# Masks first and 64-row heads in turn over two banks, in a fused attention and expert kernel on one Trainium2 core

## The chip, the cores and the metric

The kernel runs on one NeuronCore of a Trainium2 chip. The metric is the device time of one execution in microseconds (us); smaller is better. The engines are named as in the profile: PE is TensorE (PEld its weight loads), DVE is VectorE, ACT is ScalarE, POOL is GpSimd and SP is SyncE, which here issues the transfers of weights. SBUF is the memory on the core, PSUM the eight banks that PE writes its results to.

## What is computed

Two transformer blocks over 256 tokens of width 1024, in float32. The first has three attention branches on one normed input: A (8 heads of 64, each query keeps the 64 keys that a separate index scores highest), B (8 heads of 96, causal) and M (4 heads of 128, over a memory). The second has a differential attention, a gated linear attention in chunks of 64 tokens, a cross attention and a mixture of 32 experts. Cut to the parts that the change touches:

```python
# branch A: index, top 64 keys, masked attention
dots = einsum('bqhc,bsc->bhqs', q_i, k_i) * 64 ** -0.5
index = einsum('bhqs,bqh->bqs', relu(dots), w_i * 8 ** -0.5)
_, idx = top_k(where(causal, index, -1e30), 64)
p = softmax(where(kept, einsum('bqhd,bkhd->bhqk', q_a, k_a) * 64 ** -0.5, -1e30))
# linear attention, per chunk of 64 tokens
a = where(lower, einsum(q * e_pos, k * e_neg), einsum(q * e_neg, k * e_pos))
# differential attention: the mask lets a token see its own chunk of 64 and those before
p = softmax(where(mask, q1 @ k1 * s, -inf)) - lam * softmax(where(mask, q2 @ k2 * s, -inf))
```

## The kernel before

Tokens lie in two tiles of 128 rows, t = 0 and 1. Every dense product runs through one stream (`Stream`): its order is a list of names (`ORDER`), its weights come in pieces of 1 MB through SP into a pool of 23 slots, and each piece is split into a high and a low part (ACT at L165, DVE at L166) before PE multiplies it. `pump()` places one unit of that work, as a rule 12 matmuls of 512 columns (L214), and the splits of units ahead. The order of the work on each engine is the order in which the code is written: attention code calls `pump` or `fill` at fixed places to put units between its own steps, and lists such as `fills([3, 5, 1, ...])` say how many units go after each step.

An attention works on units `(t, heads, keys)`. Stage 1 (`s1`, or `d1` in the differential attention) writes the scores of a unit into one PSUM bank of 512 columns (tag `sc`, of which there are two) and calls `exps`: a maximum on DVE (L624), its negation (L625), then one exponential per head on ACT (L628). Stage 2 transposes the result on PE (L640) and copies it (L642), stage 3 multiplies it with the values (L674, L1563). A mask is added to the scores by one more matmul, the stationary `negid` (-1e30 on the diagonal) times a mask of zeros and ones (`add_mask`, L685).

Four places have a contraction of 64 rows, where a head lies either in rows 0 to 63 or in rows 64 to 127 of the operand: the index scores (`idx1`, L1093), the scores of branch A (`scores_a`, L1182), the chunk products of the linear attention (L1464), and the differential attention (`d1`, L1538, its two maps in the two halves). In the first two, `causal_units(2)` gives units whose heads all lie in one half:

```python
return [(t, hs, (t + 1) * P) for t in (1, 0) for hs in groups(8, 512 // ((t + 1) * P), step)]
```

`scores_a` and `d1` write one head's scores and then that head's mask. Ahead of branch A, `branch_input("B", ysb)` transposes the result of branch B through both `sc` banks (L543), with evictions on ACT (L526) and DVE (L527). After the dense part come the experts: their weights pass through the same slots, four experts at a time in strips of 32 rows (L1848, L1880).

Of the kernel before, what the change touches and what calls it, by code (L numbers as in the profile page):

```python
# [322 lines left out]
def block_kernel(ctx: ExitStack, tc: tile.TileContext, a: dict, out: bass.AP):  # L323
# [308 lines left out]
    on_act = [0, 0]  # L632

# [11 lines left out]
    def attention(units, fill, scores, rs, vals, close, heads, dv, out_heads=None):  # L645
# [38 lines left out]
    def add_mask(out_ap, mask):  # L684
        PE.matmul(out_ap, lhsT=negid, rhs=mask, start=False, stop=True)  # L685
# [77 lines left out]
    chmask = masks_bf[:, 0:P]  # L763
    POOL.memset(chmask, 0.0)
    POOL.memset(chmask[0:64, 64:128], 1.0)
# [322 lines left out]
    def idx1(u):  # L1088
        t, hs, nk = u
        sc = ps([P, len(hs), nk], "sc")  # L1090
        for i, hd in enumerate(hs):
            p0 = 64 * (hd % 2)
            PE.matmul(sc[:, i, :], lhsT=qiT[p0:p0 + 64, hd // 2, t * P:(t + 1) * P],  # L1093
                      rhs=kiT[p0:p0 + 64, 0, 0:nk], start=True, stop=True)
        rl = et([P, len(hs), nk])
        on_act[1] += 2
        if on_act[1] >= 4:
            on_act[1] -= 4
            DVE.tensor_scalar(rl, sc, 0.0, None, op0=OP.max)
        else:  # L1100
            ACT.activation(rl, sc, AF.Relu)
        relus[id(u)] = rl

    def idx2(u):
        t, hs, nk = u
        rl = relus.pop(id(u))
        for i, hd in enumerate(hs):
# [29 lines left out]
    pipeline(causal_units(2), (idx1, idx2), fills([1, 0, 2, 3, 0, 2, 0]))  # L1137
# [23 lines left out]
    def scores_b(t, hd, nk, dst):  # L1161
        PE.matmul(dst, lhsT=qbT[0:96, hd, t * P:(t + 1) * P], rhs=kbT[0:96, hd, 0:nk], start=True, stop=False)
        add_mask(dst[:, nk - P:], noncausal)
# [36 lines left out]
    def scores_m(t, hd, nk, dst):  # L1200
        PE.matmul(dst, lhsT=qmT[:, hd, t * P:(t + 1) * P], rhs=kmT[:, hd, :], start=True, stop=True)
# [38 lines left out]

    lq = st([P, 4, 64], "wk")
# [213 lines left out]
    for t in range(NT):  # L1455
        aT = et([P, 2, 2, P])
        POOL.memset(aT, 0.0)
        ats[t] = aT
        for par in range(2):
            pa = ps([P, 2, 2, P], "sc")  # L1460
            p0 = 64 * par
            for f, (ki, qi) in enumerate(((3, 0), (2, 1))):
                for hp in range(2):
                    PE.matmul(pa[:, f, hp, :], lhsT=gqa[p0:p0 + 64, ki, hp, t * P:(t + 1) * P],  # L1464
                              rhs=gqa[p0:p0 + 64, qi, hp, t * P:(t + 1) * P], start=True, stop=True)
            for f, m in enumerate((mlow, mup)):
                DVE.copy_predicated(aT[:, par], m[:, None, :].to_broadcast([P, 2, P]), pa[:, f])
# [56 lines left out]

# [3 lines left out]
    def d1(u):  # L1528
# [4 lines left out]
        es = []  # L1533
# [504 lines left out]
```

## Time and profile before

| | |
|---|---|
| three runs | 1045.23, 1046.37, 1047.03 us, median 1046.37 us |
| the profiled execution | 1044.64 us, of which the span of its instructions is 1042.9 us |
| PE busy | 930.0 us (89%) |
| DVE, ACT, POOL busy | 445.5, 333.8, 112.5 us |
| mean bandwidth from memory | 278 GB/s over the span |

The span runs from the first to the last instruction; the device time has 1.7 us more around it. A matmul's busy time runs to its modelled end, which lies behind the start of the next one, so that lengths on PE are read here from start to start. The granted clock of PE is given as a share of 2.4 GHz: 1.00 is 2.4 GHz, 0.50 is 1.2 GHz. A stretch has the columns busy time (and count) for each engine, then the clock, the share of the transfer engines that is busy, and GB/s.

### The profile page before, as it was taken

How to read it: one execution, taken by the hardware profiler on the slowest of the kernel's cores; microseconds unless marked ns; L12 is line 12 of the kernel's file. 1: busy time of each engine (PE TensorE's matmuls, PEld its weight loads, DVE VectorE, ACT ScalarE, POOL GpSimd, SP SyncE). 2: the span in 40 equal slices, each digit the busy share in tenths (PEclk: the TensorE clock that was granted, in tenths of full speed). 3: DMA queues.
4: the chain of work that ended last, by engine and by line, in shares of the span. 5: the costliest groups of instructions: out<-in, count | busy, mean ns of one | idle time of the engine just before them, and what ended most of it. 6: DMA issues, size and time to landing. Idle time of an engine off the chain costs nothing.

```text
span 1042.9 us, 12833 instructions
## 1 busy us (share of the span) xinstructions
PE 930.0 (89%) x5073; PEld 622.4 (60%) x5073; DVE 445.5 (43%) x814; ACT 333.8 (32%) x637; POOL 112.5 (11%) x156
## 2 busy tenths in 40 slices
PE   8999999999999999999999999877878687787876
PEld 8978877788888887877887853413232141422323
DVE  5689775476676666766765421101000010100002
ACT  6556565355534573445654200000000000000000
POOL 4354000020132011310002000000000000000000
PEclk9999999999999999999999999989989898988978
DMA  6933344345473732463578989999999999999997
GB/s 221 385 127 120 112 152 145 117 163 166 157 228 108 231 120 94 165 219 105 200 279 293 354 332 418 420 421 418 420 419 419 421 419 420 419 419 420 420 407 241
DMA packets 88316, 289.85 MB, mean 278 GB/s; under 512 B 5841, under 2 KB 20030, under 8 KB 66750
## 3 DMA queue, kind: packets, MB, share of 16 engines
q1 hardware_dynamic: 87294, 286.46, 72.4%
q0 software_dynamic: 960, 2.55, 0.9%
q8 instruction: 41, 0.67, 0.3%
q14 instruction: 21, 0.17, 0.0%
HBM read 287.94 MB, written 1.05 MB: 277 GB/s over the span
## 4 chain that ended last, share of the span: by engine, by line
PE 51%; DMA 38%; DVE 6%; ACT 2%; SPq 1%; issue 1%; POOL 0%; ACTq 0%; POOLq 0%; DVEq 0%
PE pg L214 36%; DMA s<-in_w_e_up_dram 13%; DMA s<-in_w_e_down_dram 12%; DMA s<-in_w_e_gate_dram 11%; DVE s L166 2%; PE po L674 2%; PE psc L1848 2%; PE psc L543 1%; PE psc L1182 1%; PE ptp L640 1%; PE psc L1538 1%; SPq L143 1%; PE psc L1880 1%; DVE s L577 1%; PE psc L685 1%
## 5 line engine op out<-in xcount | busy, mean ns | idle before, releaser
L214 PE MATMUL pg<-s,s 128*128 128x512 f32 (+5 forms) x2076 | 454.2, 376 | 4.0 <-ACT s L165 1.8
L214 PEld LDWEIGHTS pg<-s,s 128*128 128x128 f32 x2076 | 365.9, 189 | 71.0 <-ACT s L165 2.5
L1848 PE MATMUL psc<-s,wk 128*32 128x512 f32 (+1 forms) x1024 | 180.0, 697 | 63.3 <-DMA s<-in_w_e_up_dram 38.9
L166 DVE TENSOR_TENSOR s<-s,s 128x1024 fp32r<-128x1024 f32 (+4 forms) x170 | 197.0, 1190 | 49.3 <-ACT s L165 49.0
L165 ACT ACTIVATE s<-s 128x1024 fp32r<-128x1024 f32 (+4 forms) x170 | 160.8, 995 | 13.0 <-DVE s L166 7.6
L1848 PEld LDWEIGHTS psc<-s,wk 128*32 128x32 f32 x1024 | 41.3, 127 | 195.2 <-issue 76.0
L1880 PE MATMUL psc<-s,wk 128*32 128x512 f32 (+1 forms) x576 | 71.0, 571 | 10.8 <-DMA s<-in_w_e_down_dram 10.4
L1855 DVE SCALAR_TENSOR_TENSOR wk<-wk,psc 128x512 f32<-128x512 f32 x8 | 5.5, 687 | 135.3 <-ACT wk L1854 135.3
L1872 ACT ACTIVATE wk<-ptp 128x512 f32<-128x512 f32 (+1 forms) x9 | 4.9, 550 | 172.4 <-PE ptp L1871 172.4
L1859 DVE TENSOR_TENSOR wk<-wk,psc 128x512 f32<-128x512 f32 (+1 forms) x8 | 5.2, 654 | 120.6 <-PE psc L1848 120.6
L628 ACT ACTIVATE s<-psc,sm,tiny 128x256 f32<-128x256 f32 (+1 forms) x64 | 32.9, 520 | 72.1 <-DVE sm L625 71.5
L494 POOL TENSOR_TENSOR sm<-sm,tiny 128x8 f32<-128x8 f32 (+2 forms) x28 | 36.0, 1299 | 179.5 <-DVE sm L498 146.4
L1880 PEld LDWEIGHTS psc<-s,wk 128*32 128x32 f32 x576 | 20.1, 116 | 55.6 <-issue 32.4
L1805 PE MATMUL ptp<-masks,h 128*128 128x128 f32 x128 | 30.3, 398 | 12.7 <-DVE masks L1792 12.7
L1805 PEld LDWEIGHTS ptp<-masks,h 128*128 128x128 f32 x128 | 28.6, 311 | 19.1 <-issue 17.5
L1854 ACT ACTIVATE wk<-psc 128x512 f32<-128x512 f32 x8 | 4.8, 597 | 109.6 <-PE psc L1848 109.6
L1885 DVE COPY wk<-psc 128x512 f32<-128x512 f32 (+1 forms) x10 | 6.1, 611 | 68.5 <-PE psc L1880 68.5
L624 DVE TENSOR_REDUCE sm<-psc 128x2 f32<-128x512 f32 (+1 forms) x26 | 17.9, 689 | 32.6 <-PE psc L685 23.6
L1892 PE MATMUL pg<-wk,wr 128*128 128x512 f32 (+1 forms) x72 | 30.2, 559 | 0.0
L1805 PE MATMUL po<-masks,h 128*128 128x128 f32 x120 | 28.2, 388 | 0.0
L1805 PEld LDWEIGHTS po<-masks,h 128*128 128x128 f32 x120 | 27.6, 320 | 0.0
L1887 ACT ACTIVATE wk<-psc 128x512 f32<-128x512 f32 (+1 forms) x8 | 4.6, 570 | 71.3 <-PE psc L1880 71.3
(328 smaller groups left out, 805.1 us busy)
## 6 DMA issues: line engine op xcount, KB each, us to landing
s<-in_w_e_gate_dram SPq DMA_DIRECT2D x64, 1024.0 KB
s<-in_w_e_up_dram SPq DMA_DIRECT2D x64, 1024.0 KB
s<-in_w_e_down_dram SPq DMA_DIRECT2D x60, 1024.0 KB
s<-in_w_in_dram SPq DMA_DIRECT2D x36, 1024.0 KB
s<-in_w_ckv_dram SPq DMA_DIRECT2D x8, 1024.0 KB
s<-in_w_branch_dram SPq DMA_DIRECT2D x6, 1024.0 KB
s<-in_w_mem_kv_dram SPq DMA_DIRECT2D x4, 1024.0 KB
s<-in_w_out_dram SPq DMA_DIRECT2D x4, 1024.0 KB
```

The source lines that it names most:

```text
L143: dma(out=self.loads[x][1][part], in_=self.loads[x][0][part])
L165: self.k.nc.scalar.activation(hl[:, 0], w, AF.Copy)
L166: self.k.nc.vector.tensor_tensor(out=hl[:, 1], in0=w, in1=hl[:, 0].bitcast(F32), op=OP.subtract)
L214: mm(j.outs[t], lhsT=x_, rhs=hl[:, int(c == 2), i, :], start=step == ends[t][0], stop=step == ends[t][1])
L494: POOL.tensor_tensor(out=dst, in0=src, in1=e_.to_broadcast(shape), op=OP.pow)
L624: DVE.tensor_reduce(out=mx, in_=sc, axis=AX.X, op=OP.max)
L628: ACT.activation(e[:, i, :], sc[:, i, :], AF.Exp, bias=nb[:, i:i + 1], scale=rs[:, c:c + 1], accum_out=sums[:, c:c + 1])
L674: PE.matmul(o[:, hd % (out_heads or heads), :], lhsT=pt[:, i * nkt + kt, :], rhs=vals(kt, hd), start=(kt == 0), stop=(kt == nkt - 1))
L1805: PE.matmul(tp[:, kb - k0, :], lhsT=src, rhs=sel[:, t], start=(t == 0), stop=(t == 1))
L1848: PE.matmul(p_[s0:s0 + sn, :], lhsT=xs[k0 // 4][:, kb, s0:s0 + sn], rhs=rows(m, i, k0 + kb, cols), start=(k0 + kb == 0), stop=(k0 + kb == 7))
L1880: PE.matmul(p_[s0:s0 + sn, :], lhsT=hT[:, kb, s0:s0 + sn], rhs=rows(2, i, kb, slice(c * 512 + cols.start, c * 512 + cols.stop)), start=(kb ...
L1892: PE.matmul(outs[t][c], lhsT=sgT[:, t, :], rhs=od, start=start, stop=stop)
```

## The change

Index scores: the heads of a pair of units lie in the two halves, and each matmul goes to the other unit's bank than the one before it. Branch A: the same pairing; the mask of a whole bank is written first by one matmul of 512 columns, and the scores are added to it; two units of weight products are placed between the transposes of branch B's result and the first mask, and the numbers of units between the steps are others. Linear attention: the two halves in turn, into two banks. Differential attention: both masks first, over all keys in place of the last 128, then the scores of the two maps in turn. The chunk mask, now of 256 columns, is built by POOL after branch M in place of at the start. In the other attentions the scores functions take another form with the same matmuls.

```diff
-    def add_mask(out_ap, mask):
-        PE.matmul(out_ap, lhsT=negid, rhs=mask, start=False, stop=True)
+    def begin_mask(out_ap, mask):
+        n, nk = out_ap.shape[1:]
+        PE.matmul(out_ap, lhsT=negid, rhs=mask[:, None, :].to_broadcast([P, n, nk]), start=True, stop=False)
+
+    def in_turn(banks):
+        for i in range(len(banks[0])):
+            for b, items in enumerate(banks):
+                yield b, i, items[i], i + 1 == len(items)
...
         def s1(u):
-            t, hs, nk = u
+            if index[id(u)] % at_once:
+                return
+            us = units[index[id(u)]:index[id(u)] + at_once]
+            t, _, nk = u
...
-            sc = ps([P, len(hs), nk], "sc")
-            for i, hd in enumerate(hs):
-                scores(t, hd, nk, sc[:, i, :])
-            live[id(u)] = exps(sc, rs[t], hs, per_t[t][1])
+            scs = [ps([P, len(hs), nk], "sc") for _, hs, _ in us]
+            scores(t, [hs for _, hs, _ in us], nk, scs)
+            for x_, sc in zip(us, scs):
+                live[id(x_)] = exps(sc, rs[t], x_[1], per_t[t][1])
...
-    chmask = masks_bf[:, 0:P]
-    POOL.memset(chmask, 0.0)
-    POOL.memset(chmask[0:64, 64:128], 1.0)
...
+    def paired_units():
+        for t in (1, 0):
+            n = 4 // (t + 1)
+            for h0 in range(0, 8, 2 * n):
+                for par in range(2):
+                    yield t, list(range(h0 + par, h0 + 2 * n, 2)), (t + 1) * P
...
-    pipeline(causal_units(2), (idx1, idx2), fills([1, 0, 2, 3, 0, 2, 0]))
+    pu = list(paired_units())
+    pipeline([pu[i:i + 2] for i in range(0, len(pu), 2)], (idx1, idx2), fills([2, 2, 2, 2]))
...
-    def scores_a(t, hd, nk, dst):
-        p0 = 64 * (hd % 2)
-        PE.matmul(dst, lhsT=qaT[p0:p0 + 64, hd // 2, t * P:(t + 1) * P], rhs=kaT[p0:p0 + 64, hd // 2, 0:nk],
-                  start=True, stop=False)
-        add_mask(dst, amask[t][:, 0:nk])
+    def scores_a(t, banks, nk, outs):
+        for o in outs:
+            begin_mask(o, amask[t][:, 0:nk])
+        for b, i, hd, end in in_turn(banks):
+            p0 = 64 * (hd % 2)
+            PE.matmul(outs[b][:, i, :], lhsT=qaT[p0:p0 + 64, hd // 2, t * P:(t + 1) * P],
+                      rhs=kaT[p0:p0 + 64, hd // 2, 0:nk], start=False, stop=end)
 
     branch_input("B", ysb)
+    begun_at = W.next_mm
+    while W.next_mm < begun_at + 2:
+        fill()
+
...
-    attention(causal_units(2), fills([3, 5, 1, 1, 2, 4, 0, 2]), scores_a, rs_a, values_a,
-              closer(ysa, pair_of("zya", 0), 8, 64, r1), 8, 64)
+    attention(list(paired_units()), fills([3, 2, 3, 1, 3, 2, 0, 1]), scores_a, rs_a, values_a,
+              closer(ysa, pair_of("zya", 0), 8, 64, r1), 8, 64, at_once=2)
...
+    chmask = masks_bf[:, 0:S]
+    POOL.memset(chmask, 0.0)
+    POOL.memset(chmask[0:64, S - 64:], 1.0)
...
+        pas = [ps([P, 2, 2, P], "sc") for _ in range(2)]
+        pieces = [(f, hp, ki, qi) for f, (ki, qi) in enumerate(((3, 0), (2, 1))) for hp in range(2)]
+        for par, _, (f, hp, ki, qi), _ in in_turn([pieces, pieces]):
+            p0 = 64 * par
+            PE.matmul(pas[par][:, f, hp, :], lhsT=gqa[p0:p0 + 64, ki, hp, t * P:(t + 1) * P],
+                      rhs=gqa[p0:p0 + 64, qi, hp, t * P:(t + 1) * P], start=True, stop=True)
...
-        es = []
-        for m in range(2):
-            sc = ps([P, n, nk], "sc")
+        hs = list(range(h0, h0 + n))
+        scs = [ps([P, n, nk], "sc") for _ in range(2)]
+        for sc in scs:
+            begin_mask(sc, chmask[:, S - nk:])
+        for m, i, hd, end in in_turn([hs, hs]):
             p0 = 64 * m
-            for i in range(n):
-                PE.matmul(sc[:, i, :], lhsT=dqT[p0:p0 + 64, h0 + i, t * P:(t + 1) * P],
-                          rhs=dkT[p0:p0 + 64, h0 + i, 0:nk], start=True, stop=False)
-                add_mask(sc[:, i, nk - P:], chmask)
-            es.append(exps(sc, rs_d[t][:, m:8:2], list(range(h0, h0 + n)), dsum[t][:, m, :]))
+            PE.matmul(scs[m][:, i, :], lhsT=dqT[p0:p0 + 64, hd, t * P:(t + 1) * P], rhs=dkT[p0:p0 + 64, hd, 0:nk],
+                      start=False, stop=end)
+        es = [exps(scs[m], rs_d[t][:, m:8:2], hs, dsum[t][:, m, :]) for m in range(2)]
```

On PE at the start of branch A, before: `s_199` is branch B's result, `psc` the score banks, `pg` the product banks, and a trailing number tells one buffer from another.

```order
L543 MATMUL psc_1639<-ident,s_199_1151 128x128 x4
L543 MATMUL psc_1644<-ident,s_199_1151 128x128 x4
L1182 MATMUL psc_1659<-s_168_1026 128x256
L685 LDWEIGHTS negid
L685 MATMUL psc_1659<-masks,negid 128x256
L1182 MATMUL psc_1659<-s_168_1026 128x256
L685 LDWEIGHTS negid
L685 MATMUL psc_1659<-masks,negid 128x256
L214 MATMUL pg_1675<-s_273_1566,s_269_1537 128x512 x3
L214 MATMUL pg_1676<-s_273_1566,s_269_1537 128x512 x3
```

In the changed kernel, from the last rows of the second of two product units that now stand between those transposes and the first mask (its last operand `s_269` is the memory, as in the last rows above):

```order
L214 MATMUL pg_1661<-s_278_1601,s_269_1535 128x512 x3
L214 MATMUL pg_1662<-s_278_1601,s_269_1535 128x512 x3
L688 LDWEIGHTS negid
L688 MATMUL psc_1693<-masks,negid 128x512
L688 LDWEIGHTS negid
L688 MATMUL psc_1694<-masks,negid 128x512
L1198 MATMUL psc_1693<-s_168_1024 128x256
L1198 MATMUL psc_1694<-s_168_1024 128x256
L1198 MATMUL psc_1693<-s_168_1024 128x256
L1198 MATMUL psc_1694<-s_168_1024 128x256
```

The product units that stood behind the first scores are ahead of them, and four heads share one visit to the score banks.

On PE at the first unit of the differential attention, before: `s_635` holds its queries and keys.

```order
L1538 MATMUL psc_4104<-s_635_3836 128x256
L685 LDWEIGHTS negid
L685 MATMUL psc_4104<-masks,negid 128x128
L1538 MATMUL psc_4104<-s_635_3836 128x256
L685 LDWEIGHTS negid
L685 MATMUL psc_4104<-masks,negid 128x128
L1538 MATMUL psc_4115<-s_635_3836 128x256
L685 LDWEIGHTS negid
L685 MATMUL psc_4115<-masks,negid 128x128
```

The same place in the changed kernel:

```order
L688 LDWEIGHTS negid
L688 MATMUL psc_4094<-masks,negid 128x512
L688 LDWEIGHTS negid
L688 MATMUL psc_4095<-masks,negid 128x512
L1561 MATMUL psc_4094<-s_635_3826 128x256
L1561 MATMUL psc_4095<-s_635_3826 128x256
L1561 MATMUL psc_4094<-s_635_3826 128x256
L1561 MATMUL psc_4095<-s_635_3826 128x256
L214 MATMUL pg_4065<-s_668_3996,s_383_2177 128x512 x3
L214 MATMUL pg_4066<-s_668_3996,s_383_2177 128x512 x3
```

Both masks come first and the scores alternate. As before, one unit of twelve product matmuls, of which the first two rows stand here, separates this unit from the next, whose two masks need both banks again.

## Rows read from the trace of the kernel before

**Rows 1.** The page: busy time of PE, share of the span, instructions.

```profile
PE 930.0 (89%) x5073; PEld 622.4 (60%) x5073; DVE 445.5 (43%) x814; ACT 333.8 (32%) x637; POOL 112.5 (11%) x156
```

**Rows 2.** Stretches of the span: PE, PEld, DVE, ACT, POOL, clock, transfers, GB/s.

```profile
480.00:612.00 132.00, 127.25 (x749) 101.76 (x752) 75.33 (x166) 58.66 (x132) 10.96 (x18) 1.00 0.73 261
612.00:1042.00 430.00, 333.36 (x1912) 132.03 (x1904) 42.75 (x80) 16.75 (x32) 0.00 (x0) 0.90 1.00 409
```

**Rows 3.** SP's waits from 480 to 613 us: total, times, longest.

```profile
SPq L135 <- PE pg L214: 61.1, 15, 8.1
...
SPq L135 <- DMA s<-in_w_e_gate_dram: 0.2, 1, 0.2
```

**Rows 4.** Timeline of PE at the index scores: start, length, engine, line.

```profile
51.12 1.13 PE L1093 MATMUL psc<-s,s 64*128 64x256 f32 x4
52.18 3.01 PE L214 MATMUL pg<-s,s 128*128 128x512 f32 x12
55.12 1.14 PE L1093 MATMUL psc<-s,s 64*128 64x256 f32 x8
56.26 5.79 PE L214 MATMUL pg<-s,s 128*128 128x512 f32 x24
...
63.04 8.45 PE L214 MATMUL pg<-s,s 128*128 128x512 f32 x36
71.42 1.71 PE L1093 MATMUL psc<-s,s 64*128 64x128 f32 x16
73.06 0.64 PE L590 MATMUL ptp<-ident,s 128*96 128x128 f32 x4
```

**Rows 5.** Timeline of PE at branch A; in brackets its idle time before.

```profile
153.01 1.03 PE L543 MATMUL psc<-ident,s 128*128 128x128 f32 x8
156.07 0.67 PE L1182 MATMUL psc<-s 64*128 64x256 f32 x2 [2.03 <-DVE s L527]
...
157.96 9.60 PE L214 MATMUL pg<-s,s 128*128 128x512 f32 x36
167.49 0.70 PE L1182 MATMUL psc<-s 64*128 64x256 f32 x2
...
169.07 0.60 PE L640 MATMUL ptp<-ident,s 128*128 128x128 f32 x4
...
194.80 0.48 PE L1182 MATMUL psc<-s 64*128 64x128 f32 x2
...
197.01 0.61 PE L640 MATMUL ptp<-ident,s 128*128 128x128 f32 x4
```

**Rows 6.** A stretch of branch A, with the clock behind POOL's column.

```profile
157.04:160.45 3.41, 3.41 (x9) 2.28 (x10) 0.85 (x2) 1.12 (x5) 0.00 (x0) 0.50 0.23 84
```

**Rows 7.** Timeline of DVE and of PE at the linear attention's chunk products.

```profile
414.07 1.72 DVE L1467 COPY_PREDICATED s<-s,psc 128x256 f32<-128x256 int32 x4 [1.79 <-PE psc L1464]
...
412.80 1.71 PE L1464 MATMUL psc<-s 64*128 64x128 f32 x16
415.13 1.93 PE L1464 MATMUL psc<-s 64*128 64x128 f32 x16 [0.61 <-DVE s L1467]
416.99 1.30 PE L1473 MATMUL po<-s,s 128*128 128x128 f32 x10
```

**Rows 8.** Timeline of all engines at the differential attention.

```profile
466.71 0.67 PE L1538 MATMUL psc<-s 64*128 64x256 f32 x2 [0.62 <-DVE s L577]
...
468.36 0.69 DVE L624 TENSOR_REDUCE sm<-psc 128x2 f32<-128x512 f32 x1 [1.80 <-PE psc L685]
...
469.34 0.56 ACT L628 ACTIVATE s<-psc,sm,tiny 128x256 f32<-128x256 f32 x1 [2.38 <-DVE sm L625]
...
469.71 3.01 PE L214 MATMUL pg<-s,s 128*128 128x512 f32 x12
...
471.92 0.20 ACT L628 ACTIVATION_READ_ACCUMULATOR s<-psc,sm,tiny 128x1 f32 x1
...
478.99 0.48 PE L1538 MATMUL psc<-s 64*128 64x128 f32 x2
...
483.50 0.61 PE L640 MATMUL ptp<-ident,s 128*128 128x128 f32 x4
```

**Rows 9.** Timeline of PE in the cross attention.

```profile
551.61 1.56 PE L1618 MATMUL psc<-s,s 128*128 128x256 f32 x6 [1.79 <-ACT s L579]
```

More of the change, by code (lines that the diff above doesn't have):

```diff
@@ L643, in weights_T, with attention @@
         return pt
-    def attention(units, fill, scores, rs, vals, close, heads, dv, out_heads=None):
+    def attention(units, fill, scores, rs, vals, close, heads, dv, out_heads=None, at_once=1):
         live = {}
@@ L1086, in causal_units, with idx1, idx2 @@
         return [(t, hs, (t + 1) * P) for t in (1, 0) for hs in groups(8, 512 // ((t + 1) * P), step)]
[L1088 to L1091, printed above, removed]
+    def paired_units():
[4 more added lines that the diff above has]
+                    yield t, list(range(h0 + par, h0 + 2 * n, 2)), (t + 1) * P
+    def idx1(us):
+        t, nk = us[0][0], us[0][2]
+        scs = [ps([P, len(hs), nk], "sc") for _, hs, _ in us]
+        for b, i, hd, _ in in_turn([hs for _, hs, _ in us]):
             p0 = 64 * (hd % 2)
-            PE.matmul(sc[:, i, :], lhsT=qiT[p0:p0 + 64, hd // 2, t * P:(t + 1) * P],
+            PE.matmul(scs[b][:, i, :], lhsT=qiT[p0:p0 + 64, hd // 2, t * P:(t + 1) * P],
                       rhs=kiT[p0:p0 + 64, 0, 0:nk], start=True, stop=True)
[L1095 to L1107, printed above, removed]
+        relus[id(us)] = [et([P, len(hs), nk]) for _, hs, _ in us]
+        ACT.activation(relus[id(us)][0], scs[0], AF.Relu)
+        DVE.tensor_scalar(relus[id(us)][1], scs[1], 0.0, None, op0=OP.max)
+    def idx2(us):
+        t, nk = us[0][0], us[0][2]
+        rls = relus.pop(id(us))
+        for b, i, hd, _ in in_turn([hs for _, hs, _ in us]):
+            rl = rls[b]
             w_ = wi[:, t, hd:hd + 1]
@@ L1159, in block_kernel, with scores_b @@
     qbT, kbT, vb = place["qbT"], place["kbT"], pair_of("vbz", 0)
-    def scores_b(t, hd, nk, dst):
-        PE.matmul(dst, lhsT=qbT[0:96, hd, t * P:(t + 1) * P], rhs=kbT[0:96, hd, 0:nk], start=True, stop=False)
-        add_mask(dst[:, nk - P:], noncausal)
+    def scores_b(t, banks, nk, outs):
+        for _, i, hd, _ in in_turn(banks):
+            dst = outs[0][:, i, :]
+            PE.matmul(dst, lhsT=qbT[0:96, hd, t * P:(t + 1) * P], rhs=kbT[0:96, hd, 0:nk], start=True, stop=False)
+            PE.matmul(dst[:, nk - P:], lhsT=negid, rhs=noncausal, start=False, stop=True)
     def values_b(kt, hd):
@@ L1198, in block_kernel, with scores_m @@
     kmT, qmT, vm = place["kqm"][:, 0], place["kqm"][:, 1], pair_of("vzm", 0)
-    def scores_m(t, hd, nk, dst):
-        PE.matmul(dst, lhsT=qmT[:, hd, t * P:(t + 1) * P], rhs=kmT[:, hd, :], start=True, stop=True)
+    def scores_m(t, banks, nk, outs):
+        for _, i, hd, _ in in_turn(banks):
+            PE.matmul(outs[0][:, i, :], lhsT=qmT[:, hd, t * P:(t + 1) * P], rhs=kmT[:, hd, :], start=True, stop=True)
     attention([(t, hs, S) for t in range(NT) for hs in groups(4, 2, 1)], fills([3, 0, 3, 1, 1, 4]), scores_m, rs_m,
@@ L1458, in block_kernel @@
         ats[t] = aT
-        for par in range(2):
[L1460 to L1465, printed above, removed]
+        pas = [ps([P, 2, 2, P], "sc") for _ in range(2)]
[4 more added lines that the diff above has]
+                      rhs=gqa[p0:p0 + 64, qi, hp, t * P:(t + 1) * P], start=True, stop=True)
+        for par in range(2):
             for f, m in enumerate((mlow, mup)):
-                DVE.copy_predicated(aT[:, par], m[:, None, :].to_broadcast([P, 2, P]), pa[:, f])
+                DVE.copy_predicated(aT[:, par], m[:, None, :].to_broadcast([P, 2, P]), pas[par][:, f])
     for t in range(NT):
@@ L1614, in block_kernel, with scores_x @@
     ox = {}
-    def scores_x(t, hd, nk, dst):
-        for b in range(2):
-            PE.matmul(dst, lhsT=qxT[:, 2 * hd + b, t * P:(t + 1) * P], rhs=kxT[:, 2 * hd + b, :],
-                      start=(b == 0), stop=(b == 1))
+    def scores_x(t, banks, nk, outs):
+        for _, i, hd, _ in in_turn(banks):
+            for b in range(2):
+                PE.matmul(outs[0][:, i, :], lhsT=qxT[:, 2 * hd + b, t * P:(t + 1) * P], rhs=kxT[:, 2 * hd + b, :],
+                          start=(b == 0), stop=(b == 1))
     def close_x(t, hs, o, sums):
```

1 line of the change is left out of this document (removed).

## The prediction

> **What bounds the kernel now.** I began with the page, for the engine that is never free: PE is busy for 930 of 1042.9 us [rows 1]. Cut into stretches, the span has two regimes [rows 2]. From 480 to 612 us PE works 127 of 132 us at full clock while the transfer engines are busy 73%; from 612 us on, those engines are busy all the time, at 409 GB/s, and PE is not. So the first part is PE's, the second belongs to the experts' weights. Whether time saved early reaches the end is read from SP's waits before 613 us [rows 3]: SP waits for PE's products, 61.1 us in total, and for an earlier transfer only 0.2. Weights are fetched when PE frees a slot, so if PE reaches 612 us earlier by x, the saturated stretch begins and ends earlier by x. A change on PE is therefore worth what it moves PE's clockwork before 612 us, no more. For that I read PE's timeline from start to start, and beside it DVE and ACT, since a score bank is free only after its exponentials.
>
> **Term 1, the index scores.** A unit of four matmuls of 256 columns, all in one half, lasts from 51.12 to the product at 52.18, 1.06 us. Where two units of different halves stand next to each other, eight of them last from 55.12 to 56.26, 1.14 us [rows 4]: the halves work at the same time, and PE already does this by itself where the code lets it. The last two units, sixteen matmuls of 128 columns, last from 71.42 to 73.06, 1.64. With the other single unit (like the first) the present cost is 1.06 + 1.14 + 1.06 + 1.64 = 4.9 us. Afterwards there are three visits, each of two halves: 3 x 1.14 = 3.4. I take **-1.5 us**; if the last pair stays at 1.64 it is -1.0, and as a product after a visit starts slowly too and one visit goes, -2.0 is the other end.
>
> The Trainium skill, page "TensorE: Matmul & The Clock Gate", section "Part 3: Packing small matmuls", says that matmuls start and end strictly in program order. These rows differ: the code has all of one half first, yet both halves finish together. By the rule the present kernel would have no overlap here, and this term would be about 1 us larger, the time 1032 us.
>
> **Term 2, branch A.** Three things go.
> - The gap. After the transposes of branch B's result PE stands still for 2.03 us, until DVE has emptied the last score bank [rows 5]. The change puts two product units there (twelve matmuls each, 8.38 / 3 = 2.8 us by the 36 from 63.04 to 71.42 [rows 4]). Their weights were split before the gap, since they run right after the first scores now. -2.0; 0 if they wait after all.
> - The clock. Right behind that gap the granted clock is 0.50, that is 1.2 GHz, for 3.41 us [rows 6]; the 36 product matmuls from 157.96 take 9.53 us [rows 5] where the same number takes 8.38 [rows 4]. With the gap filled I expect no fall: -1.2, or 0. A gap of 1.79 us in the cross attention [rows 9] stands in a stretch at 1.00 [rows 2].
> - The masks and the halves. The units cost 1.89 (156.07 to 157.96), three times 1.58 (167.49 to 169.07, two more like it), and twice 2.21 (194.80 to 197.01 and its like) [rows 5]: 11.05 us. A unit of 1.58 is four scores of 1.06 as above and 0.52 for its masks and changes of shape. Afterwards a pair of units has two masks of 512 columns and eight scores. The mask columns are as many as before (8 x 256 + 8 x 128 = 6 x 512), so two masks cost at most 2 x 0.52, and at least two streams of 512 columns, 2 x 0.23 by the product rows; near the lower end, 0.55, since one change of shape is left of several. With 1.14 for the scores a pair costs 1.7, three pairs 5.1. **-5.9**, between -4.5 (dear masks) and -6.4.
>
> No new wait follows here: between two pairs stand five and four product units, 14 and 11 us, while four exponentials take ACT about 3 us (below) and a split 1. Where the list now holds 2 + 15 units in place of 18, one unit runs later and nothing is saved or lost. Branch A together: **-9.1 us**.
>
> **Term 3, the linear attention.** Sixteen matmuls of each tile of tokens shrink as above, but PE is not what sets the pace. DVE's four copies begin at 414.07, when the first bank is done, and take 1.72 [rows 7]. The second tile needs both banks at once: its second half cannot start before the fourth copy ends at 415.8, and then needs about 1.1 us, to 416.9. Now the next matmul starts at 416.99. So **0**: PE's gain turns into a wait of some 1.9 us in place of 0.61. Bounds: -1.2 if nothing waits (3.6 us of scores [rows 7] against two visits of 1.2), +1.7 if the wait halves the clock for one stretch as in [rows 6].
>
> **Term 4, the differential attention.** The first unit takes 466.71 to 469.71, 3.0 us, the second the same within 0.1, the third 478.99 to 483.50, 4.5 [rows 8]: 10.5 us, against three pairs of 1.7 by term 2 (the wider masks are in that). On PE alone that is -5.4. But only one product unit of 2.8 us stands between two visits, and each visit now wants both banks. The exponentials start at 469.34 and end at 472.12 [rows 8]; the maximum before them starts at 468.36, and both banks would be written by 468.4, so this chain begins no earlier than now. PE would be back at 466.71 + 1.7 + 2.8 = 471.2 and wait some 1.3 us for the second bank. The second visit's chain also begins where DVE is free, as now, so there is a like wait before the third, and 0.6 us at the single transpose bank. Of 5.4 about 2.6 goes into these waits: **-2.8 us**, between 0 (the chain takes all) and -5.4 (no wait).
>
> The Trainium skill, page "TensorEngine Tiling (Array Packing)", section "PSUM Bottleneck", speaks against the change: tiling speeds up TensorE, but not the emptying of PSUM. Rows 7 and 8 agree with it in these two places; rows 5 do not show it in branch A.
>
> **What costs nothing.** The two POOL fills of the chunk mask move behind branch M; POOL is busy 11% of the span [rows 1], and the last mask matmul of branch A, which they overwrite, is long past. Scores of branches B, M and of the cross attention are the same instructions.
>
> **Sum.** -1.5 - 9.1 + 0 - 2.8 = -13.4 us. The profiled execution took 1044.64 us, 1.7 more than its span, and is 1.7 below the median of the runs shown, so 1031.2 on its scale is **1033.0 us** on that of the median. Small ends: -1.0 - 4.5 + 1.7 + 0 = -3.8, or 1042.6. Large ends: -2.0 - 9.6 - 1.2 - 5.4 = -18.2, or 1028.2.
>
> **The rivals.**
> - Banks bind in branch A too: PE arrives at both banks before the exponentials have left them, and the 5.9 there shrinks as the 5.4 did, to about half, with term 4 at half of its 2.8: 13.4 - 3.0 - 1.4 = 9.0, some less if the filled gap reappears before the first mask; 1037 to 1040 us. For it: both banks of two are claimed at once. Against: 11 us and more of products between the pairs.
> - Slower: turning between the halves costs what a change of shape costs. Now two units of 0.52 hold two masks each; their 512 columns stream in 0.23, which leaves 0.14 for each mask's going and coming. The new code turns at every score, 64 times (16 in each of the four places). Without overlap branch A would give 3.3 for its masks and 3.2 for gap and clock, the differential attention 3, the index scores and chunks would lose 1.3: -8.2. At 0.14 a turn 64 turns cost 9.0, and it breaks even near 0.13; at 0.2 it ends 4.6 slower, 1051 us. Against it: eight in 1.14 us [rows 4].
> - The freed time does not reach the end because the weights come no sooner: 1045 to 1047. Against it stand SP's waits [rows 3].
> - More than forecast: no wait in terms 3 and 4, 1029 us. Against it: only one product unit between the visits.
>
> **How the numbers follow.** About 0.2% (2 us) is what a measurement of this kernel can tell from no change. Forecast with its bounds 0.66, banks binding in branch A 0.18, more than forecast 0.07, nothing reaching the end 0.05, slower 0.04. The first three are all faster by over 2 us: 0.91; same 0.05; slower 0.04. The likeliest case is 1033.0. From 1029.0 to 1041.0 lie the forecast with most of its bounds, the first rival and the lower edge of the fourth, some 0.85; I leave the last 0.05 for terms that I have not seen.
>
> **What would show it.** Right: no stretch at half clock at branch A, and products in place of the 2.03 us gap; eight scores in 1.1 to 1.2 us in the index, branch A and the differential attention; PE idle for one to two microseconds before the second and third visit of the latter, and for about 2 before the second tile of the linear attention; the saturated stretch of transfers beginning 12 to 15 us earlier than 612 us and as long as before. Wrong: scores of two halves one after the other, PE waiting for a score bank in branch A, or PE early at 590 us and the stream of weights no earlier.

## The result, and the profile after

The changed kernel takes 1032.61 us (median of four runs, 1031.90 to 1034.28), the kernel before 1046.28 (four runs, 1045.23 to 1047.03): a ratio of 0.9869, with a 95% interval from 0.9836 to 0.9901. The forecast was 1033.0, between 1029.0 and 1041.0. The two profiled executions lie closer together than the medians: 1044.64 us before (span 1042.9), below the lowest of its four runs, and 1034.28 after (span 1032.6), its longest run. About 3 us of the changed kernel's profiled time lie in two stretches at half clock, below; whether its other executions have them too is not shown. One of E6's six runs below took 1260.51 us, at a mean granted clock of 0.645; without it E6's median is 1031.69 in place of 1031.75.

The page of the changed kernel, busy time by engine, which answers to [rows 1]:

```profile
PE 911.8 (88%) x5053; PEld 614.5 (60%) x5053; DVE 445.3 (43%) x814; ACT 333.4 (32%) x637; POOL 113.7 (11%) x156
```

The two microseconds in which the transfer engines become busy, first in the kernel before, with the columns of [rows 2]:

```profile
605.00:607.00 2.00, 2.00 (x21) 0.53 (x17) 0.35 (x1) 0.00 (x0) 0.00 (x0) 1.00 0.75 295
```

The same in the changed kernel, and its saturated stretch:

```profile
595.00:597.00 2.00, 2.00 (x24) 0.65 (x20) 0.00 (x0) 0.00 (x0) 0.00 (x0) 1.00 0.95 401
602.00:1032.00 430.00, 326.61 (x1908) 131.32 (x1900) 42.77 (x80) 16.77 (x32) 0.00 (x0) 0.92 1.00 408
```

SP's waits from 470 to 603 us, as in [rows 3]:

```profile
SPq L135 <- PE pg L214: 54.2, 14, 6.6
```

PE's busy time fell by 18 us, of which 7 lie in the saturated stretch (333.4 to 326.6 us), where PE does not set the pace. In the 5 us ahead of the windows shown, the transfer engines are busy 9% before and 10% after, so they saturate some 10 us earlier. The end of the span comes 10.3 us earlier too, and the saturated stretch is as long as in [rows 2], 430 us at 408 GB/s: what PE gains ahead of it reaches the end, as the forecast said. SP still waits for PE's products there.

Where the time went is read from the start of the same PE instruction in both traces. The shift is after minus before.

| stage | before, from and to | after, from and to | change in the stage |
|---|---|---|---|
| index scores | 51.12, 73.06 | 51.15, 72.68 | -0.4 |
| branch A, to the first score of branch M | 153.01, 238.67 | 152.59, 228.70 | -9.5 |
| linear attention, to its next product unit | 412.80, 419.09 | 402.85, 410.68 | +1.5 |
| differential attention, to the cross attention | 466.71, 543.67 | 458.22, 531.35 | -3.8 |
| cross attention, to its second transposes | 543.67, 553.45 | 531.35, 542.73 | +1.6 |
| the rest, to the end of the span | 553.45, 1042.9 | 542.73, 1032.6 | +0.4 |

Timeline of the changed kernel at the index scores, on PE:

```profile
51.15 1.13 PE L1107 MATMUL psc<-s,s 64*128 64x256 f32 x8
52.22 3.01 PE L214 MATMUL pg<-s,s 128*128 128x512 f32 x12
56.29 3.06 PE L214 MATMUL pg<-s,s 128*128 128x512 f32 x12 [1.06 <-ACT s L915]
59.28 1.14 PE L1107 MATMUL psc<-s,s 64*128 64x256 f32 x8
66.01 1.16 PE L1107 MATMUL psc<-s,s 64*128 64x128 f32 x16
```

The same on ACT, the first evictions after that visit:

```profile
55.41 0.46 ACT L913 ACTIVATE s<-pg,tiny 128x256 f32<-128x256 f32 x1
55.77 0.47 ACT L915 ACTIVATE s<-pg,tiny 128x256 f32<-128x256 f32 x1
```

The three visits take 1.07, 1.06 and 1.09 us (3.2; the four of before took 4.9), but a new wait of 1.06 us has come between the two product units after the first visit. The second unit needs a product bank that ACT begins to empty only at 55.41. Before, ACT began to empty that bank at nearly the same time, 55.38, but the visit at 55.12 [rows 4] lay across that moment, and PE went on at 56.26 without a wait.

Timeline of PE at branch A:

```profile
153.38 5.70 PE L214 MATMUL pg<-s,s 128*128 128x512 f32 x24
158.92 0.60 PE L688 MATMUL psc<-masks,negid 128*128 128x512 bf16 x2
159.45 1.13 PE L1198 MATMUL psc<-s 64*128 64x256 f32 x8
160.52 8.46 PE L214 MATMUL pg<-s,s 128*128 128x512 f32 x36
...
190.05 0.60 PE L688 MATMUL psc<-masks,negid 128*128 128x512 bf16 x2
190.59 1.16 PE L1198 MATMUL psc<-s 64*128 64x128 f32 x16
191.68 0.66 PE L638 MATMUL ptp<-ident,s 128*128 128x128 f32 x4
```

The stretch of [rows 6], with the clock behind POOL's column:

```profile
157.04:160.45 3.41, 3.41 (x19) 2.15 (x18) 1.68 (x2) 0.24 (x1) 0.00 (x0) 1.00 0.92 283
```

The gap of 2.03 us in [rows 5] is filled, no stretch is at half clock, and a pair takes 1.60 us (158.92 to 160.52): 0.53 for two masks and 1.07 for eight scores. The three pairs take 1.60, 1.60 and 1.63, together 4.8 in place of 11.05. No wait for a bank stands anywhere in branch A.

Timeline of PE and DVE at the linear attention:

```profile
402.85 1.16 PE L1486 MATMUL psc<-s 64*128 64x128 f32 x16
404.11 1.72 DVE L1490 COPY_PREDICATED s<-s,psc 128x256 f32<-128x256 int32 x4 [1.79 <-PE psc L1486]
405.18 0.46 PE L1486 MATMUL psc<-s 64*128 64x128 f32 x2 [1.16 <-DVE s L1490]
405.98 1.70 PE L1486 MATMUL psc<-s 64*128 64x128 f32 x14 [0.35 <-DVE s L1490]
407.61 2.27 PE L1496 MATMUL po<-s,s 128*128 128x128 f32 x10
```

The two stretches at half clock that the changed kernel has between 14 and 600 us:

```profile
406.36:409.77 3.41, 3.41 (x23) 2.96 (x21) 1.66 (x4) 0.00 (x0) 0.00 (x0) 0.50 0.25 39
539.48:542.89 3.41, 3.41 (x9) 2.59 (x10) 0.17 (x1) 0.85 (x3) 3.38 (x5) 0.50 1.05 387
```

PE waits 1.16 us for DVE's copies of the first bank and 0.35 for those of the second, and right behind that the clock is at 0.50 for 3.41 us. The other fall stands behind the gap of 1.8 us in the cross attention, which [rows 9] has too, there at full clock.

Timeline of PE at the differential attention, with the last exponential of the first visit on ACT:

```profile
458.22 0.77 PE L688 MATMUL psc<-masks,negid 128*128 128x512 bf16 x2 [0.53 <-DVE s L577]
458.92 1.13 PE L1561 MATMUL psc<-s 64*128 64x256 f32 x8
...
462.71 0.56 ACT L628 ACTIVATE s<-psc,sm,tiny 128x256 f32<-128x256 f32 x1
462.84 0.39 PE L688 MATMUL psc<-masks,negid 128*128 128x512 bf16 x1
463.41 0.38 PE L688 MATMUL psc<-masks,negid 128*128 128x512 bf16 x1 [0.19 <-ACT s L628]
468.04 0.39 PE L688 MATMUL psc<-masks,negid 128*128 128x512 bf16 x1
469.13 0.38 PE L688 MATMUL psc<-masks,negid 128*128 128x512 bf16 x1 [0.70 <-ACT s L628]
471.10 0.66 PE L638 MATMUL ptp<-ident,s 128*128 128x128 f32 x4 [0.51 <-DVE s L640]
```

The waits are where the forecast put them, at the second bank of the second and third visit and at the transpose bank, but they are 0.2, 0.7 and 0.5 us long.

### The profile page after: what moved, and what is told of

Read it like the earlier page. It is cut to its first block, busy times and chain, and to the rows that moved or that the text cites. A ratio compares the mean times of both kernels' runs of the same rounds, so it can differ in the third digit from the quotient of the medians.

```text
span 1032.6 us, 12784 instructions
## 1 busy us (share of the span) xinstructions
PE 911.8 (88%) x5053; PEld 614.5 (60%) x5053; DVE 445.3 (43%) x814; ACT 333.4 (32%) x637; POOL 113.7 (11%) x156
## 3 DMA queue, kind: packets, MB, share of 16 engines
q1 hardware_dynamic: 87294, 286.46, 73.1%
## 4 chain that ended last, share of the span: by engine, by line
PE 49%; DMA 38%; DVE 8%; ACT 2%; SPq 1%; issue 1%; POOL 0%; ACTq 0%; POOLq 0%; DVEq 0%
PE pg L214 36%; DMA s<-in_w_e_up_dram 13%; DMA s<-in_w_e_down_dram 12%; DMA s<-in_w_e_gate_dram 12%; DVE s L166 2%; PE psc L1871 2%; PE po L675 2%; PE psc L543 1%; ACT s L628 1%; DVE s L577 1%; PE ptp L638 1%; PE psc L1641 1%; PE psc L1903 1%; SPq L143 1%; PE ptp L1828 1%
## 5 line engine op out<-in xcount | busy, mean ns | idle before, releaser
L1871 PE MATMUL psc<-s,wk 128*32 128x512 f32 (+1 forms) x1024 | 172.3, 660 | 67.2 <-DMA s<-in_w_e_up_dram 43.2
L1903 PE MATMUL psc<-s,wk 128*32 128x512 f32 (+1 forms) x576 | 71.9, 559 | 12.9 <-DMA s<-in_w_e_down_dram 12.6
```

The costliest lines, as they stand in the source:

```text
L1871: PE.matmul(p_[s0:s0 + sn, :], lhsT=xs[k0 // 4][:, kb, s0:s0 + sn], rhs=rows(m, i, k0 + kb, cols), start=(k0 + kb == 0), stop=(k0 + kb == 7))
L1903: PE.matmul(p_[s0:s0 + sn, :], lhsT=hT[:, kb, s0:s0 + sn], rhs=rows(2, i, kb, slice(c * 512 + cols.start, c * 512 + cols.stop)), start=(kb ...
```

## The experiments

Each is one edit of the changed kernel (E1: of the kernel before). E1 to E4 were measured together, E0 and E5 to E7 together, and E8 and E9 together. From one such group to the next the median of the same kernel moves by one to two microseconds (the kernel before 1046.02 to 1047.94, the changed kernel 1032.61 and 1033.74), so that small things are read from the traces. For E1 to E4 the changed kernel stands in another group, at 1032.61.

**E1, the product units ahead, alone.**

```diff
     branch_input("B", ysb)
+    begun_at = W.next_mm
+    while W.next_mm < begun_at + 2:
+        fill()
...
-    attention(causal_units(2), fills([3, 5, 1, 1, 2, 4, 0, 2]), scores_a, rs_a, values_a,
+    attention(causal_units(2), fills([3, 3, 1, 1, 2, 4, 0, 2]), scores_a, rs_a, values_a,
```

> The kernel before, with only the two product units put ahead of branch A's first scores and taken from the five behind the second unit. Theory: the gap of 2.03 us and the stretch at half clock behind it (1.2 us) go and the units keep their lengths (1.58, 2.21 us): 3.2 us less than before, about 1043. Rival one: the gap only moves, since the units taken from between the scores no longer cover the exponentials; a like gap of 1 to 2 us stands before a transpose, and the gain is 1 to 2 us. Rival two: the fall of the clock was not the gap's; a stretch at half clock stays in branch A and the gain is 2.0.

Measured: 1041.74 us against 1046.62 for the kernel before in the same group, ratio 0.996 (0.9942 to 0.9979): 4.9 us less by the medians, 4.2 by the ratio. Timeline of PE at branch A in E1:

```profile
159.86 0.70 PE L1182 MATMUL psc<-s 64*128 64x256 f32 x2
...
161.37 8.47 PE L214 MATMUL pg<-s,s 128*128 128x512 f32 x36
```

The gap and the half clock are gone from branch A, and the first unit takes 1.51 us where it took 1.89. From the transposes to 70 us later the trace gives 4.0 us; up to 0.46 of it is another wait, ahead of the transposes at 226.0 us, that is no longer in the trace. The other 3.6 are the gap (2.0), the clock on the 36 products (1.1) and the clock on the first unit (0.4), which the theory had left out. No gap moved elsewhere, so the theory stands. The profiled execution also has a stretch at half clock from 478.30 to 485.13 us, in the differential attention. PE's last idle time ahead of it ended 15 us earlier, and the kernel before ran the same code at full clock; so this fall has no gap at all, and the gain is read from branch A alone.

**E7, the changed kernel without the units ahead.**

```diff
     branch_input("B", ysb)
-    begun_at = W.next_mm
-    while W.next_mm < begun_at + 2:
-        fill()
...
-    attention(list(paired_units()), fills([3, 2, 3, 1, 3, 2, 0, 1]), scores_a, rs_a, values_a,
+    attention(list(paired_units()), fills([5, 2, 3, 1, 3, 2, 0, 1]), scores_a, rs_a, values_a,
```

> The changed kernel without the two product units ahead of branch A (five units behind the first pair in place of three). Theory: PE waits for branch B's last eviction again, 2.0 us ahead of the first mask, so 2.0 us slower than the changed kernel, 3.2 where the half clock comes with the gap, as in the kernel before. Rival: with masks first the wait matters less, since the first mask needs one bank only and the scores wait for the second: the gap shrinks to 1.2 us or less.

Measured: 1035.30 us, 1.6 more than the changed kernel in the same group (E0). Timeline of PE behind the gap:

```profile
154.87 0.94 PE L688 MATMUL psc<-masks,negid 128*128 128x512 bf16 x2 [1.94 <-DVE s L527]
...
157.75 14.30 PE L214 MATMUL pg<-s,s 128*128 128x512 f32 x60
```

The stretch that begins there, with its clock:

```profile
155.17:158.58 3.41, 3.41 (x12) 2.02 (x12) 0.70 (x2) 0.00 (x0) 0.00 (x0) 0.50 0.41 155
```

The gap comes back with 1.94 us, and the half clock with it; the first pair takes 2.88 us in place of 1.60. From the transposes to the first score of branch M E7 takes 3.1 us more than the changed kernel, 3.65 without a wait for a transfer that only the latter has (0.59 us). The medians show less than the 3.2 us that were expected; in the profiled execution E7's linear attention runs at full clock, which takes off 1.5 (E0). In the two kernels that have this gap, the clock fell behind it; in the ten others that were profiled, it did not fall here. The rival that masks first would shorten the gap falls.

**E3, masks first but halves apart, in branch A.**

```diff
-    attention(list(paired_units()), fills([3, 2, 3, 1, 3, 2, 0, 1]), scores_a, rs_a, values_a,
-              closer(ysa, pair_of("zya", 0), 8, 64, r1), 8, 64, at_once=2)
+    attention(causal_units(2), fills([3, 3, 1, 1, 2, 4, 0, 2]), scores_a, rs_a, values_a,
+              closer(ysa, pair_of("zya", 0), 8, 64, r1), 8, 64)
```

> The changed kernel with branch A's units unpaired again (one half, one bank at a time), each with one mask of 512 columns first. It splits the saving of branch A's score units (11.05 us before, 4.8 now) into masks and halves. Theory: a unit of 256 columns takes 1.06 for its scores and 0.4 for its mask, a unit of 128 columns 1.1 and 0.4: 4 x 1.46 + 2 x 1.5 = 8.8, so 4.0 us slower than the changed kernel (3.4 to 4.5): two thirds of the saving are the halves'. Rival: the masks' changes of shape were the larger part: units of 1.1 to 1.2, 1.5 to 2 us slower than the changed kernel.

Measured: 1036.49 us, 3.9 more than the changed kernel. Timeline of PE in E3, one unit of each width:

```profile
169.23 0.39 PE L688 MATMUL psc<-masks,negid 128*128 128x512 bf16 x1
169.55 1.13 PE L1198 MATMUL psc<-s 64*128 64x256 f32 x4
170.61 0.66 PE L638 MATMUL ptp<-ident,s 128*128 128x128 f32 x4
...
190.35 0.39 PE L688 MATMUL psc<-masks,negid 128*128 128x512 bf16 x1
190.67 1.16 PE L1198 MATMUL psc<-s 64*128 64x128 f32 x8
191.76 0.66 PE L638 MATMUL ptp<-ident,s 128*128 128x128 f32 x4
```

A unit takes 1.38 (256 columns) or 1.41 us (128 columns): 4 x 1.38 + 2 x 1.41 = 8.3. Of the 6.2 us that the units give, 0.4 are the clock's (the first unit, 1.89 - 1.51 in E1), 10.7 - 8.3 = 2.3 the masks' and 8.3 - 4.8 = 3.5 the halves'. Four scores of one half take the 1.06 us that eight of both halves take.

**E2, both banks and masks first, but one half after the other.**

```diff
-        for i in range(len(banks[0])):
-            for b, items in enumerate(banks):
+        for b, items in enumerate(banks):
+            for i in range(len(items)):
                 yield b, i, items[i], i + 1 == len(items)
```

> The changed kernel with both banks claimed and the masks first, but all scores of one half before those of the other, in all four places. Theory (PE runs the two halves beside each other whatever the order, some four matmuls ahead): the visits of eight scores of 256 columns stay at 1.07 us, those of sixteen of 128 columns go from 1.1 to 1.6; there are five such, of which the two of the linear attention lie beside a wait: 1 to 1.5 us slower than the changed kernel. Rival one, the strict order: visits of 256 columns take 2.1 us, those of 128 columns 2.0, ten visits, 8 to 10 us slower. Rival two, a turn costs time: visits become shorter, 1 us or more faster.

Measured: 1033.56 us, 0.95 more than the changed kernel, which is no more than groups differ by; the trace decides. Timeline of PE in E2, one visit of each width:

```profile
160.97 1.14 PE L1198 MATMUL psc<-s 64*128 64x256 f32 x8
162.04 8.46 PE L214 MATMUL pg<-s,s 128*128 128x512 f32 x36
...
192.12 1.71 PE L1198 MATMUL psc<-s 64*128 64x128 f32 x16
193.76 0.66 PE L638 MATMUL ptp<-ident,s 128*128 128x128 f32 x4
```

Eight scores of 256 columns still take 1.07 us, sixteen of 128 columns 1.64 where the changed kernel takes 1.09. So what matters is that both banks are claimed and both halves stand side by side in the order; turning at every matmul adds only in the narrow visits. A turn costs nothing that can be seen. PE does not wait for one half to be done before it begins the other: the eight starts of E2's wide visit come in pairs 0.01 us apart, as in the changed kernel, where four scores of one half alone start 0.2 to 0.3 us apart. Of the sixteen narrow ones, four start alone before the other half joins.

**E4, the differential attention as before.**

```diff
-        for sc in scs:
-            begin_mask(sc, chmask[:, S - nk:])
-        for m, i, hd, end in in_turn([hs, hs]):
...
+        for m in range(2):
+            sc = ps([P, n, nk], "sc")
+            p0 = 64 * m
+            for i in range(n):
+                PE.matmul(sc[:, i, :], lhsT=dqT[p0:p0 + 64, h0 + i, t * P:(t + 1) * P],
+                          rhs=dkT[p0:p0 + 64, h0 + i, 0:nk], start=True, stop=False)
+                PE.matmul(sc[:, i, nk - P:], lhsT=negid, rhs=chmask[:, S - P:], start=False, stop=True)
```

> The changed kernel with the differential attention as before (each score followed by its mask, one bank after the other). Theory: the trace's saving there, 3.8 us, comes back and reaches the end: 3.8 us slower than the changed kernel, and no idle time of PE before the second mask of a visit. Rival: what is saved there is given back by 612 us in other waits: within 1 us of the changed kernel.

Measured: 1037.40 us, 4.8 more than the changed kernel. The profiled execution has a stretch at half clock from 460.0 us and none in the cross attention, which shifts its parts. From the first scores here to the cross attention E4 takes 78.5 us and the changed kernel 73.1; of these 5.4 us that stretch is 1.5, which leaves 3.9. The sign and size agree, and the rival (given back by 612 us) falls.

**E0, the changed kernel again,** with no edit.

> The changed kernel once more, nothing edited. Two stretches at half clock stand in its first profile ahead of 600 us: at 406.4 us in the linear attention and at 539.5 in the cross attention, each some 1.5 us of loss; the kernel before had neither, with gaps as long. Theory: they fall in some executions and not in others, so here at least one is missing or another stands elsewhere, while every stage at full clock keeps its length to 0.1 us; the span without the two would be 1029.5. Rival: they belong to the code (the longer wait in the linear attention, the earlier cross attention): both come again within 1 us of their places.

Measured: 1033.74 us (1031.74 to 1034.49). Both stretches at half clock came again, at 407.3 and 540.4 us. My theory that they come and go by the execution is not borne out by this pair; the rival's forecast came true. In the linear attention a fall stands in four of the five profiles that have its waits of 1.16 and 0.35 us (the changed kernel twice, E3 and E4), and in none of the five with one wait of 0.61 or 0.62 (the kernel before, E1, E2, E5 and E8). Yet neither fall is bound to its gap alone: E7 has the waits of 1.16 and 0.35 us, with the stretch from 407 to 410 at 1.00, and the 1.8 us in the cross attention stand in all kernels, with the clock at 1.00 behind them in the kernel before, E1, E4, E5, E6, E8 and E9, and at 0.50 in the changed kernel (twice), E2, E3 and E7. What decides stays open.

**E5, the linear attention as before.**

```diff
-        pas = [ps([P, 2, 2, P], "sc") for _ in range(2)]
...
+        for par in range(2):
+            pa = ps([P, 2, 2, P], "sc")
+            p0 = 64 * par
+            for f, (ki, qi) in enumerate(((3, 0), (2, 1))):
+                for hp in range(2):
+                    PE.matmul(pa[:, f, hp, :], lhsT=gqa[p0:p0 + 64, ki, hp, t * P:(t + 1) * P],
+                              rhs=gqa[p0:p0 + 64, qi, hp, t * P:(t + 1) * P], start=True, stop=True)
```

> The changed kernel with the linear attention's chunk products as before (one bank after the other). Theory (DVE's copies set the pace there): the wait before the second tile is 0.6 us in place of 1.16, the visits are 1.65 in place of 1.1, and from the first chunk product to the first product with the values it takes 4.2 us, as in the kernel before; the changed form takes 4.2 at full clock as well, so the pairing there is worth 0 to 0.3 us, plus what a fall of the clock behind the longer wait costs in the executions that have one. Rival: the pairing itself slows this place by over 0.5 us at full clock.

Measured: 1031.01 us, 2.7 less than the changed kernel in the same group. Timeline of PE in E5, the first chunk products and the first product with the values:

```profile
401.68 1.71 PE L1487 MATMUL psc<-s 64*128 64x128 f32 x16
...
405.86 1.30 PE L1496 MATMUL po<-s,s 128*128 128x128 f32 x10
```

The same in E7, which has the changed form, at full clock:

```profile
405.24 1.16 PE L1483 MATMUL psc<-s 64*128 64x128 f32 x16
...
409.43 1.30 PE L1493 MATMUL po<-s,s 128*128 128x128 f32 x10
```

The stage takes 4.18 us in E5 and 4.19 in E7. So the pairing is worth nothing here at full clock, and E5 has the shorter wait (0.61 us) with no fall of the clock behind it. Its profile has no fall in the cross attention either, so the 2.7 us are not the linear attention's alone.

**E6, product units at the three waits.**

```diff
-    pipeline([pu[i:i + 2] for i in range(0, len(pu), 2)], (idx1, idx2), fills([2, 2, 2, 2]))
+    pipeline([pu[i:i + 2] for i in range(0, len(pu), 2)], (idx1, idx2), fills([1, 3, 2, 2]))
...
+        if t == 0:
+            pump()
     for t in range(NT):
         aT = ats[t]
...
-        pump(2)
+        pump(1 + t)
     k.give(5)
...
-    pipeline([(1, 0, 2), (1, 2, 2), (0, 0, 4)], (d1, d2, d3), pumps([1, 1, 3, 2, 3]))
+    pipeline([(1, 0, 2), (1, 2, 2), (0, 0, 4)], (d1, d2, d3), pumps([2, 2, 1, 2, 3]))
```

> The changed kernel with product units at the three places where PE waits for a bank: index fills 1, 3, 2, 2 in place of 2, 2, 2, 2; one unit between the two tiles of the linear attention, taken from the two behind the first tile's output; differential attention 2, 2, 1, 2, 3 in place of 1, 1, 3, 2, 3. Theory: the wait of 1.06 us in the index goes, that of 1.16 in the linear attention too, and of the waits of 0.2, 0.7 and 0.5 in the differential attention most: 3 us less than the changed kernel, about 1029.6, and more where a fall of the clock goes with them. Rival: the units are missing where they were taken from (the third visit's transposes, the first tile's output), and as long waits stand there: within 1 us of the changed kernel.

Measured: 1031.75 us, 2.0 less than the changed kernel in the same group. The three waits are gone, but two have come where the units were missing, one of 0.90 us behind the first tile's output and a longer one in the differential attention. Timeline of PE in E6:

```profile
478.23 0.71 PE L638 MATMUL ptp<-ident,s 128*128 128x128 f32 x4 [2.73 <-DVE s L640]
```

Theory and rival were both half right: the index and the linear attention gained, the differential attention gave it back in one wait of 2.73 us for DVE, which itself waited for the third visit's exponentials. A stretch at half clock follows it, from 478.70 to 482.11 us.

**E8 and E9, the units taken elsewhere.** Both have E6's index fills and 1, 2, 2, 2, 3 in the differential attention. E8 has the linear attention as before; E9 has the changed form with one unit between its tiles, taken from the two behind the second tile:

```diff
+        if t == 0:
+            pump()
...
-        pump(2)
+        pump(2 - t)
     k.give(5)
```

> The changed kernel with the linear attention as before, index fills 1, 3, 2, 2, and units 1, 2, 2, 2, 3 in the differential attention in place of 1, 1, 3, 2, 3. Theory: from the kernel that differs by the linear attention alone (1031.0 us) the index gives 1.06 and the waits before the third visit and at the transpose bank 1.2, with no gap of 2.7 at the third visit's transposes, since two units (5.7 us) cover its exponentials: about 1028.8. Rival: one unit less there leaves a gap of 1 us or more and only the index's 1.06 is won: 1030.

> The same index and differential fills, and the changed form of the linear attention with one product unit between its two tiles, taken from the two behind the second tile's output. Theory: its two visits take 1.1 us each and nothing waits: 2.2 from the first chunk product to the first with the values, product unit aside, in place of 4.2, so 2.0 less than the kernel with the old form, about 1027, and the fastest of all. Rival: the unit is missing where it was taken from, PE waits one to three microseconds ahead of the transposes of the result, and the two kernels are equal.

Measured: E8 1030.15 us, a ratio to the kernel before of 0.9854 (0.9830 to 0.9879); E9 1026.93 us, 0.9822 (0.9798 to 0.9846), the fastest of all and 3.2 less than E8. E8 won only 0.9 of the 2.2 us that were expected over E5, across two groups: a wait of 0.75 us stands at the third visit's transposes, and its profile has a stretch at half clock from 577.09 to 580.50 us that was not expected. The rival is nearer. Timeline of PE in E9:

```profile
56.99 8.49 PE L214 MATMUL pg<-s,s 128*128 128x512 f32 x36
...
401.62 1.16 PE L1486 MATMUL psc<-s 64*128 64x128 f32 x16
402.71 3.02 PE L214 MATMUL pg<-s,s 128*128 128x512 f32 x12
405.66 1.16 PE L1486 MATMUL psc<-s 64*128 64x128 f32 x16
406.75 1.30 PE L1498 MATMUL po<-s,s 128*128 128x128 f32 x10
```

In the index no unit waits any more. In the linear attention the two visits take 1.09 us each with no wait, 2.2 us in place of 4.2, as expected; of the unit taken away only 0.26 us of wait is left at the transposes of the result. That accounts for 1.7 of the 3.2 us over E8; the two profiled executions differ by 1.8, and E9's has no stretch at half clock between 15 and 600 us. Why the medians lie further apart is not shown.

## Why the prediction was right

The total came out within half a microsecond. The sign, the regime and the places of the waits are as forecast, but for one wait in the index scores. The terms are less exact than their sum: the errors of terms 1 and 4, of about one microsecond each, cancel, so that the closeness of the total is in part luck.

- **What bounds it.** Right: the saturated stretch starts earlier by what PE gained and is as long as before. In the profiled pair it starts 10 us earlier, not the 12 to 15 that were to show it, since the changed kernel's profile has two falls of the clock.
- **Term 1, the index scores: -1.5, measured -0.4.** The visits did what was said (3.2 us against a forecast of 3.4). The step that failed is that the new fills were not looked at and so cost nothing in the sum: they put two product units in a row where a visit had covered ACT's emptying of a product bank, 1.06 us. With fills of 1, 3, 2, 2 (E6, E9) it is gone.
- **Term 2, branch A: -9.1, measured -9.5.** Right part by part: the gap 2.0, the clock 1.1 on the products (9.53 to 8.4 for 36, E1), the units 6.2 in place of 5.9, since two masks cost 0.53 and a pair 1.60 to 1.63 instead of 1.7. One reading was off: the first unit's 1.89 us lie in the stretch at half clock, so 0.4 of what was booked on the masks and halves is the clock's. The large end of -6.4 there is -6.25 by its own figures (three pairs of 1.14 + 0.46), which moves only the outer bound. By E1, E7 and E3 the parts stand by themselves: 3.6 for gap and clock, 2.3 for the masks, 3.5 for the halves, 9.4 in all. The first rival, banks that bind here too, has no wait in the trace.
- **Term 3, the linear attention: 0, measured +1.5 in the profile.** At full clock it is 0 (E5 and E7, 4.18 and 4.19 us). The profiled executions of the changed kernel show the upper bound that was given, a stretch at half clock behind the wait; E7 has the same waits and no such stretch. The forecast wait of 1.9 us came as 1.16 and 0.35. The lower bound, -1.2 if nothing waits, kept the old wait of 0.61; E9, where nothing waits, takes 2.2 us, 2.0 less.
- **Term 4, the differential attention: -2.8, measured -3.8.** The mechanism was right, the size off: waits of 2.6 us were expected to come out of 5.4, and 0.2 + 0.7 + 0.5 = 1.4 came. The forecast's own figures did not give 2.6: from 471.2 to 472.12 is 0.9 us and not 1.3, and 1.3 twice with the 0.6 would be 3.2. The rest of the error is in the order: with masks first only the second mask waits for the second bank; the first mask, 0.39 us, goes into a bank that is already free. The forecast had PE wait with everything. The last exponential also ended 5.1 us after the start of the visit, where it was 5.4.
- **What was not in it.** The fall of the clock in the cross attention, 1.6 us in the profile. The four terms with the linear attention at full clock give -0.4 - 9.5 + 0 - 3.8 = -13.7, which is also the difference of the medians; with the two falls the profiled pair differs by 10.3. That the median runs are free of such falls is not shown: the changed kernel had both in each of its two profiles, and the other executions left no trace. So the agreement of the two -13.7 may be chance.
- **The rivals.** That turning costs time fell with E2. That eight scores would go one after the other fell with it: in E2 eight scores of two halves in sequence take 1.07 us, where four of one half take 1.06. The sentence of the Trainium skill, page "TensorE: Matmul & The Clock Gate", section "Part 3: Packing small matmuls", that matmuls start and end strictly in program order, does not hold in these 1.07 us. "More than forecast" was open in the kernel as it stood; E9, which puts products into the waits of terms 1, 3 and 4, ends at 1026.9. The page "TensorEngine Tiling (Array Packing)", section "PSUM Bottleneck", of the Trainium skill spoke of this limit, and the trace agrees in the linear attention: the visits shrank from 1.71 to 1.16 us, and the stage stayed at 4.2 at full clock (E7) until other work stood between them (E9).

## What to carry to other kernels

When a step on the bounding engine is made shorter, ask at once what it used to cover: here 1.1 of the 1.7 us that the index visits gained, and all that the linear attention's visits gained, went into waits for banks until a product unit was moved to cover them. Claim both banks, write the masks of a whole bank by one matmul, and let the two row halves stand next to each other; turning at every matmul is worth it for narrow ones only. When work is moved into a gap, look at how much is left where it was taken from: in the differential attention E6 left one unit and paid 2.7 us, E8 and E9 left two and paid 0.7.

## What the hardware showed that was not expected

- Two halves of rows overlap without being alternated: 1.07 us for eight scores of 256 columns either way, but 1.64 against 1.09 for sixteen of 128 columns (E2 and the changed kernel).
- The clock's falls are not bound to the length of the gap ahead of them: the cross attention's 1.8 us had a stretch at 0.50 behind them in five profiles of twelve and none in seven, with the same code around it; each costs about 1.6 us. In E1 the clock fell with no idle time of PE in the 15 us ahead. Two kernels are compared more safely by stages at full clock than by one profiled span.
